# Splitting a mixer's narrow products by output rows over the two halves of TensorE's columns

## The chip, the cores and the metric

The kernel runs on one core of one Trainium2 chip. The metric is the time of one launch in microseconds (us), as the median of several runs. A profiled execution also gives a trace: one record for every instruction on TensorE (PE for products, PEld for the loads of its stationary operand), VectorE (DVE), ScalarE (ACT), GpSimd (POOL) and SyncE (SP).

## The reference

Two blocks of two layers each work on 256 tokens of width 1024 in fp32. The first block (dilated and differential attention, then windowed attention) is not touched by the change. Each layer of the second block mixes four branches and then runs a gated feed-forward net:

```python
for layer in range(DEPTH):                       # DEPTH = 2
    h = rms_norm_2(x, norm1_g[layer])
    y_sb = stick_breaking_attention(...)         # 4 heads of 64
    y_rwkv, v_first = rwkv7_time_mix(...)        # causal, 4 heads of 64
    y_moba = moba_attention(...)
    y_hgrn = hgrn2_mixer(...)                    # causal, 4 heads of 64
    for n, y_n in enumerate((y_sb, y_rwkv, y_moba, y_hgrn)):
        merged += sigmoid(h @ w_gate[n]) * (y_n @ w_branch[layer, n])
    x = x + merged @ w_out[layer]
    h2 = rms_norm_2(x, norm2_g[layer])
    x = x + (silu(h2 @ w_ffn_gate) * (h2 @ w_ffn_up)) @ w_ffn_down
```

The two causal mixers, rwkv7 and hgrn2, are linear recurrences that are computed chunk by chunk. In rwkv7 a chunk of 128 tokens needs the inverse of a unit triangular 128x128 matrix for each head.

## The kernel before

Weights come from HBM in units of 128x1024 fp32 (`unit`, L210): SP issues the load, ACT rounds the unit to `wh` (L220), and DVE forms the rest `wl` (L221). A projection is then three TensorE products for each pair of tiles (`mm3`, L236 to L240), with a moving operand of 512 or 256 columns in the rounded type. These are the L238, L239 and L240 of the profile, and they are most of the work.

The mixers run between the projections of a layer. `mixer_layer` (L1525) weaves two generators: `Rwkv.run` on one side, and on the other the attention branches, hgrn (L1102) and their projections. A scheduler orders each engine's instructions by priority before the launch, so TensorE's order is fixed, and mixer products stand in it between groups of projection products that don't depend on them.

All mixer products are in full fp32; each such product is two records on PE and two on PEld in the trace. The ones that matter here have a stationary operand of 128x128 and a moving operand of only 64 columns (or 2):

- `Rwkv.run` inverts the triangular matrices by doubling, six levels for 2 chunks and 4 heads. One level is: `p1` (L1409, 8 products), copied by ACT to `t1` (L1410); `p3` (L1415, 8 products), merged by DVE into `Y` (L1416); then transposes of `Y` into `px` (L1422), copied by ACT to `X`.
- After it, for each chunk: `pr` (L1433), copied to `R`; `pu` (L1444), copied to `R`; `pst` (L1451, L1452) for the state, in the first chunk only; and `py` (L1463, L1465). Earlier, `pn` (L1284) and `pb` (L1315) sum over heads with 2 columns.
- hgrn builds its scores over seven levels. `hs` (L1138) is the product of a level, DVE merges it (L1140) and updates `hq` (L1148) and `key` (L1149), which the next level's `hs` reads. At the end `ho` (L1166 to L1168) applies the scores to the values, 12 products of 64 columns.

Two places of the kernel already write to one half of the output partitions at a time, with a stationary operand of 128x64: `pst`, and the value products `pv` of the attentions (L373, L987, L989). `HALF` is the pair of slices 0:64 and 64:128. Scores (L364) use 64 rows of the contraction instead.

Of the kernel before, what the change touches and what calls it, by code (L numbers as in the profile page):

```python
# [95 lines left out]
HALF = (slice(0, 64), slice(64, 128))  # L96
# [3 lines left out]
class Net:  # L100
# [50 lines left out]
    def mm(self, name="mm"):  # L151
        t = self.p_mm.tile([128, 512], F32, name=name, tag="mm")
        return t
# [195 lines left out]
    def norm_rows(self, t, g, out, done=None):  # L349

        r = self.norm_stat(t, out)
        for j in range(2):
            s = slice(j * 512, j * 512 + 512)
            self.nc.vector.scalar_tensor_tensor(out[:, s], self.x[:, t, s], r, g[:, s], op0=OP.mult, op1=OP.mult)
            if done:
                done(j, s)


    def products(self, of):

# [599 lines left out]
def zsel(ap, b, z):  # L960

    return ap.rearrange("p (n z b) -> p n z b", z=2, b=b)[:, :, z, :]
# [139 lines left out]
def hgrn(n, l, q, f, key, it, sg, yT, c0):  # L1102


    nc = n.nc
    mm = nc.tensor.matmul
    lb, om = n.lb[:, l * 2:l * 2 + 2], n.omlb[:, l * 2:l * 2 + 2]
    nom = n.nomlb[:, l * 2:l * 2 + 2]
    heads = (slice(0, 64), slice(64, 128))
    for p in range(2):  # L1110
        nc.vector.tensor_scalar(key[:, p, :], f[:, p, :], nom[:, p:p + 1], om[:, p:p + 1], op0=OP.mult, op1=OP.add)
        nc.vector.tensor_scalar(f[:, p, :], f[:, p, :], om[:, p:p + 1], lb[:, p:p + 1], op0=OP.mult, op1=OP.add)
    fl = lambda t: t.rearrange("p a b -> p (a b)")
    kf, ff = fl(key), fl(f)

    sc = n.big("scb")
    yield
    for t in range(2):
        ps = n.mx("hs")
        s = slice(t * 128, t * 128 + 128)  # L1120
        for p in range(2):
            mm(ps[:, p * 256:p * 256 + 256].rearrange("p (a b) -> p a b", a=2), lhsT=key[:, p, s], rhs=q[:, p, :, s],
               start=True, stop=True)
        nc.vector.tensor_tensor(v4(sc[:, t * 512:t * 512 + 512]), v4(ps), bc(n.ident.unsqueeze(1), [128, 4, 128]),
                                op=OP.mult)
    for par, r in enumerate(heads):
        nc.vector.tensor_mul(q[r, :, par, :], q[r, :, par, :], f[r, :, :])
    yield
    tot, b = ff, 1
    for lv in range(7):  # L1130

        ps = n.mx("hs")
        for t in range(2):
            s = slice(t * 128, t * 128 + 128)
            for p in range(2):
                o = ps[:, t * 256 + p * 128:t * 256 + p * 128 + 128]
                qz = q[:, p, :, s].rearrange("p a (n z b) -> p a n z b", z=2, b=b)[:, :, :, 1, :]
                mm(o.rearrange("p (a n b) -> p a n b", a=2, b=b), lhsT=key[:, p, s], rhs=qz, start=True, stop=True)  # L1138
        m = bc(zsel(n.msk[:, lv, :], b, 1).unsqueeze(1), [128, 8, 64 // b, b])
        nc.vector.copy_predicated(sc.rearrange("p (g n z b) -> p g n z b", g=8, z=2, b=b)[:, :, :, 1, :], m,  # L1140
                                  ps.rearrange("p (g n b) -> p g n b", g=8, b=b))
        nb = 512 // (2 * b)
        kv = kf.rearrange("p (n z c) -> p n z c", z=2, c=b)
        tv = tot.rearrange("p (n z) -> p n z", z=2)
        for par, r in enumerate(heads):
            qv = q[r, :, par, :].rearrange("p g (n z c) -> p g n z c", z=2, c=b)[:, :, :, 1, :]
            tp = tv[r, :, 0:1].rearrange("p (g n) z -> p g n z", g=2)
            nc.vector.tensor_tensor(qv, qv, bc(tp, [64, 2, nb // 2, b]), op=OP.mult)  # L1148
        nc.vector.tensor_tensor(kv[:, :, 0, :], kv[:, :, 0, :], bc(tv[:, :, 1:2], [128, nb, b]), op=OP.mult)  # L1149
        nt = n.s2("tot", tag="tot")[:, :nb]  # L1150
        nc.vector.tensor_tensor(nt, tv[:, :, 0], tv[:, :, 1], op=OP.mult)
        tot, b = nt, 2 * b
        yield
    scx = n.s2("scx", tag="tm")
    ps = n.mx("hs")
    for p in range(2):
        mm(ps[:, p * 256:p * 256 + 256].rearrange("p (a b) -> p a b", a=2), lhsT=key[:, p, 0:128],
           rhs=q[:, p, :, 128:256], start=True, stop=True)
    nc.scalar.copy(scx, ps)
    yield  # L1160
    po = n.mx("ho")
    for h in range(4):
        o0, o1 = po[:, h * 64:h * 64 + 64], po[:, 256 + h * 64:256 + h * 64 + 64]
        c = slice(h * 64, h * 64 + 64)
        hs = slice(h * 128, h * 128 + 128)
        mm(o0, lhsT=sc[:, hs], rhs=it[:, 0, c], start=True, stop=True)  # L1166
        mm(o1, lhsT=scx[:, hs], rhs=it[:, 0, c], start=True, stop=False)
        mm(o1, lhsT=sc[:, 512 + h * 128:640 + h * 128], rhs=it[:, 1, c], start=False, stop=True)  # L1168
    o = n.s2("ho", tag="tm")
    nc.scalar.copy(o, po)  # L1170
    sq = n.s2("hsq", tag="tm")
    nc.scalar.activation(sq, po, AF.Square)
    yield
    ss = n.col(8, "ss")
    nc.vector.tensor_reduce(ss, sq.rearrange("p (a b) -> p a b", a=8), axis=AX.X, op=OP.add)
    r = n.rstd(ss, 64, 1e-6, 8)
    ov = o.rearrange("p (a b) -> p a b", a=8)
    nc.vector.tensor_tensor(ov, ov, bc(r.unsqueeze(2), [128, 8, 64]), op=OP.mult)
    nc.vector.tensor_mul(o, o, sg)
    with n.lazily(LATE):  # L1180
        for t in range(2):
            n.to_T(o[:, t * 256:t * 256 + 256], t, yT, c0, 2)
    yield


class Rwkv:
# [25 lines left out]
    def run(self, yT, c0):  # L1212
        n, nc, l = self.n, self.n.nc, self.l
        mm = nc.tensor.matmul
        col = lambda name, p: n.ccol(name, l * 2 + p, 1)
        r, k, v, wag = (self.x[i] for i in range(4))
# [7 lines left out]
        for p in range(2):  # L1224
            s = slice(p * 256, p * 256 + 256)
            c = slice(p * 128, p * 128 + 128)
# [9 lines left out]
        for t in range(2):  # L1236
            mm(pg[:, t * 256:t * 256 + 256], lhsT=lw[:, 1, t * 128:t * 128 + 128], rhs=self.wa[:, 256:512],
               start=True, stop=True)
# [6 lines left out]
        else:  # L1245
# [11 lines left out]
            for p in range(2):  # L1257
                s = slice(p * 256, p * 256 + 256)
                mm(pvm[:, s], lhsT=v12[0:32, 64 + p * 128:64 + p * 128 + 128], rhs=vl[0:32, 0:256],
                   start=True, stop=True)  # L1260
# [7 lines left out]
        for t in range(2):  # L1268
            for p in range(2):
                o = t * 256 + p * 128  # L1270
                nc.tensor.transpose(pvt[:, o:o + 128], v[:, p, t * 128:t * 128 + 128], n.ident)
        vt = n.s2("vt", tag="rl")
# [6 lines left out]
        sq = n.s2("kksq", tag="rt")  # L1279
        nc.scalar.activation(sq, flat(kk), AF.Square)  # L1280
        pn = n.mx("pn")
        for t in range(2):
            for p in range(2):
                mm(pn[:, t * 4 + p * 2:t * 4 + p * 2 + 2], lhsT=sq[:, p * 256 + t * 128:p * 256 + t * 128 + 128],  # L1284
                   rhs=n.cst[:, C_HALVES:C_HALVES + 128:64], start=True, stop=True)
        yield
        rn = n.col(8, "rn")
# [24 lines left out]
        pb = n.mx("pb")  # L1312
        for t in range(2):
            for p in range(2):
                mm(pb[:, t * 4 + p * 2:t * 4 + p * 2 + 2], lhsT=bn[:, p, t * 128:t * 128 + 128],  # L1315
                   rhs=n.cst[:, C_HALVES:C_HALVES + 128:64], start=True, stop=True)
        bon = n.col(8, "bon")
        nc.vector.tensor_copy(bon, pb[:, 0:8])
# [82 lines left out]
        for lv in range(1, 7):  # L1401

            z = 1 << lv
            half = lambda t, h: t[:, h * 64:h * 64 + 64].rearrange("p (n b) -> p n b", b=z)
            p1 = {}
            for c in range(2):
                p1[c] = n.mx("p1")
                for h in range(4):
                    mm(half(p1[c], h), lhsT=aT(c, h), rhs=zsel(X[c][:, hd(h)], z, 0), start=True, stop=True)  # L1409
                nc.scalar.copy(zsel4(t1[c], z, 0), run4(p1[c][:, 0:256], z))  # L1410
            yield
            for c in range(2):
                p3 = n.mx("p3")
                for h in range(4):
                    mm(half(p3, h), lhsT=t1[c][:, hd(h)], rhs=zsel(Y[c][:, hd(h)], z, 1), start=True, stop=True)  # L1415
                nc.vector.copy_predicated(zsel4(Y[c], z, 1), mask4(n, lv, z, 1), run4(p3[:, 0:256], z))  # L1416
            yield
            if lv < 6:
                for c in range(2):
                    px = n.mx("px")  # L1420
                    for h in range(4):
                        nc.tensor.transpose(px[:, hd(h)], Y[c][:, hd(h)], n.ident)  # L1422
                    nc.scalar.copy(X[c], px)
                yield
# [4 lines left out]
        for c in range(2):  # L1429

            pr_ = n.mx("pr")
            for h in range(4):
                mm(pr_[:, h * 64:h * 64 + 64], lhsT=aTk(c, h), rhs=vt[:, c * 256 + h * 64:c * 256 + h * 64 + 64],  # L1433
                   start=(h == 0), stop=(h == 3 and c == 0), skip_group_check=True)
            if c:
                for p in range(2):
                    mm(pr_[:, p * 128:p * 128 + 128], lhsT=ar[c][:, p * 256:p * 256 + 128],
# [3 lines left out]
            nc.scalar.copy(R[:, 0:256], pr_[:, 0:256])  # L1441
            pu = n.mx("pu")
            for h in range(4):
                mm(pu[:, h * 64:h * 64 + 64], lhsT=Y[c][:, hd(h)], rhs=R[:, h * 64:h * 64 + 64], start=True, stop=True)  # L1444
            nc.scalar.copy(R[:, 256:512], pu[:, 0:256])
            if c == 0:
                pst = n.mx("pst")
# [12 lines left out]
            py = n.mx("py")  # L1460
            for h in range(4):
                o = py[:, h * 64:h * 64 + 64]
                mm(o, lhsT=bT(c, h), rhs=R[:, 256 + h * 64:320 + h * 64], start=(h == 0), stop=False,  # L1463
                   skip_group_check=True)
                mm(o, lhsT=bTk(c, h), rhs=vt[:, c * 256 + h * 64:c * 256 + h * 64 + 64], start=False,  # L1465
                   stop=(h == 3 and c == 0), skip_group_check=True)
            if c:
                for p in range(2):
                    mm(py[:, p * 128:p * 128 + 128], lhsT=ar[c][:, p * 256 + 128:p * 256 + 256],
# [257 lines left out]
```

## Time and profile before

| | |
|---|---|
| median of 3 runs | 1330.22 us (1329.13 to 1332.9) |
| the profiled execution, own time | 1330.19 us |
| its span, first to last instruction | 1328.4 us |
| PE busy | 1270.1 us, 96% |
| PEld busy | 1082.6 us, 81% |
| DVE, ACT, POOL busy | 850.6 (64%), 645.3 (49%), 67.9 us (5%) |
| mean granted TensorE clock | 0.984 |

A record on PE lasts longer than it keeps the engine from the next one, because products are pipelined; what a product costs is read from the distance between starts. Times in a timeline are in us from the span's start, and a row may merge several records of one line, with their count behind the x.

### The profile page before, as it was taken

Reading aid. Unit: us, or ns where it says so; the run is one execution under the profiler, and the core shown is the slowest. Engines: PE = TensorE matmul, PEld = TensorE weight load, DVE = VectorE, ACT = ScalarE, POOL = GpSimd, SP = SyncE. Lnnn points to the kernel's source line nnn. Section 1 sums busy time; section 2 is a strip of 40 time slices with the busy share of each in tenths; the row PEclk is TensorE's granted clock in tenths of the full one; section 3 lists DMA queues with packets and bytes.
Section 4 is the critical chain, followed back from the end, with each engine's and each line's share of the span. In section 5 each row is a group of like instructions: output and inputs, shape, how many; then the busy total and the mean of one; then the engine's idle time right before and its main releaser. Section 6 shows DMA issues by size and latency. Waiting matters only on the chain.

```text
span 1328.4 us, 20159 instructions
## 1 busy us (share of the span) xinstructions
PE 1270.1 (96%) x7760; PEld 1082.6 (81%) x7760; DVE 850.6 (64%) x1456; ACT 645.3 (49%) x1083; POOL 67.9 (5%) x82
## 2 busy tenths in 40 slices
PE   6988889999899999999999999999999999999997
PEld 4857667977797888888899987987888887999986
DVE  6876897676758765666655544658754756655543
ACT  3353545675665335445544443555345544644432
POOL 0011110000001000000000000001000000000000
PEclk8989999999999999999999999999999999999999
DMA  8977755654563314365566654653232564666652
GB/s 318 328 249 263 244 178 184 209 156 128 150 191 96 98 59 133 115 203 180 177 191 185 186 183 155 211 163 95 80 109 67 169 199 156 206 185 181 190 185 86
DMA packets 104957, 227.19 MB, mean 171 GB/s; under 512 B 8207, under 2 KB 8351, under 8 KB 104861
## 3 DMA queue, kind: packets, MB, share of 16 engines
q1 hardware_dynamic: 102560, 219.18, 52.9%
q0 software_dynamic: 1984, 6.60, 1.8%
q8 instruction: 61, 1.00, 0.3%
q14 instruction: 36, 0.29, 0.1%
q10 hardware_dynamic: 316, 0.12, 0.0%
HBM read 224.82 MB, written 1.05 MB: 170 GB/s over the span
## 4 chain that ended last, share of the span: by engine, by line
PE 75%; DVE 5%; issue 5%; DMA 2%; ACT 2%; POOL 1%; DVEq 0%; POOLq 0%; ACTq 0%
PE mm L240 20%; PE mm L238 20%; PE mm L239 20%; DMA aw<-in_ada_w_dram 2%; PE p L1409 2%; PE p L1415 2%; PE hs L1138 1%; PE sc L364 1%; DVE wl L221 1%; PE pv L373 1%; DVE macc L447 1%; ACT wh L220 1%; PE pt L393 1%; PE px L1422 1%; PE cm L364 1%
## 5 line engine op out<-in xcount | busy, mean ns | idle before, releaser
L221 DVE TENSOR_TENSOR wl<-wr,wh 128x1024 fp32r<-128x1024 f32 (+1 forms) x372 | 430.9, 1165 | 266.0 <-ACT wh L220 262.6
L220 ACT CAST wh<-wr 128x1024 fp32r<-128x1024 f32 (+1 forms) x372 | 369.9, 1003 | 400.1 <-PE mm L240 164.2
L238 PE MATMUL mm<-hh,wh 128*128 128x256 f32 x1168 | 333.7, 287 | 0.9 <-ACT hh L321 0.9
L239 PE MATMUL mm<-hl,wh 128*128 128x256 f32 x1168 | 333.9, 286 | 0.0
L240 PE MATMUL mm<-hh,wl 128*128 128x256 f32 x1168 | 332.7, 285 | 0.0
L238 PEld LDWEIGHTS mm<-hh,wh 128*128 128x128 f32 x1168 | 225.4, 194 | 4.5 <-issue 2.4
L239 PEld LDWEIGHTS mm<-hl,wh 128*128 128x128 f32 x1168 | 225.4, 193 | 2.4 <-issue 2.2
L240 PEld LDWEIGHTS mm<-hh,wl 128*128 128x128 f32 x1168 | 225.3, 193 | 2.4 <-issue 2.3
L240 PE MATMUL mm<-wh,hl 128*128 128x512 f32 (+1 forms) x448 | 177.4, 396 | 0.3 <-DVE hl L322 0.3
L238 PE MATMUL mm<-wh,hh 128*128 128x512 f32 (+1 forms) x448 | 177.1, 396 | 0.6 <-ACT hh L321 0.4
L239 PE MATMUL mm<-wl,hh 128*128 128x512 f32 (+1 forms) x448 | 176.2, 393 | 0.4 <-DVE wl L221 0.4
L238 PEld LDWEIGHTS mm<-wh,hh 128*128 128x128 f32 x448 | 85.0, 190 | 18.0 <-ACT hh L321 1.3
L239 PEld LDWEIGHTS mm<-wl,hh 128*128 128x128 f32 x448 | 85.1, 190 | 17.6 <-DVE wl L221 0.8
L240 PEld LDWEIGHTS mm<-wh,hl 128*128 128x128 f32 x448 | 85.0, 190 | 17.0 <-DVE hl L322 1.2
L239 PE MATMUL mm<-wl,ff 128*128 128x512 f32 x176 | 69.5, 395 | 0.0
L238 PE MATMUL mm<-wh,ff 128*128 128x512 f32 x176 | 69.5, 395 | 0.0
L240 PE MATMUL mm<-wh,ff 128*128 128x512 f32 x176 | 69.4, 395 | 0.0
L447 DVE SCALAR_TENSOR_TENSOR macc<-aw,cs,macc 128x512 f32<-128x512 f32 x78 | 57.3, 745 | 13.7 <-DMA aw<-in_ada_w_dram 13.1
L239 PE MATMUL mm<-wl,yTh 128*128 128x512 f32 x128 | 50.9, 399 | 2.0 <-DVE wl L221 2.0
L240 PE MATMUL mm<-wh,yTl 128*128 128x512 f32 x128 | 50.5, 396 | 0.0
L238 PE MATMUL mm<-wh,yTh 128*128 128x512 f32 x128 | 50.0, 394 | 0.0
L384 ACT ACTIVATE p<-p,nm 128x256 f32<-128x256 f32 (+1 forms) x80 | 39.6, 496 | 18.7 <-DVE nm L381 18.1
(392 smaller groups left out, 1617.3 us busy)
## 6 DMA issues: line engine op xcount, KB each, us to landing
wr<-in_w_in_dram SPq DMA_DIRECT2D x120, 512.0 KB, 3.8
wr<-in_gu_dram SPq DMA_DIRECT2D x88, 512.0 KB, 3.8
wr<-in_w_ffn_down_dram SPq DMA_DIRECT2D x44, 512.0 KB, 3.7
aw<-in_ada_w_dram SPq DMA_DIRECT2D x80, 256.0 KB, 4.5
wr<-in_ab_w_in_dram SPq DMA_DIRECT2D x32, 512.0 KB, 5.3
wr<-in_c_w_in_dram SPq DMA_DIRECT2D x20, 512.0 KB, 4.1
wr<-in_w_branch_dram SPq DMA_DIRECT2D x16, 512.0 KB, 3.8
wr<-in_w_out_dram SPq DMA_DIRECT2D x16, 512.0 KB, 3.9
```

The costliest lines, as they stand in the source:

```text
L220: nc.scalar.copy(hi[:, i:i + m], raw[:, i:i + m])
L221: nc.vector.tensor_sub(lo[:, i:i + m], raw[:, i:i + m], hi[:, i:i + m].bitcast(F32))
L238: mm(out, lhsT=ah, rhs=bh, start=start, stop=False, **kw)
L239: mm(out, lhsT=ah, rhs=bl, start=False, stop=False, **kw)
L240: mm(out, lhsT=al, rhs=bh, start=False, stop=stop, **kw)
L364: self.nc.tensor.matmul(out, lhsT=lhsT, rhs=rhs, start=True, stop=True)
L373: self.nc.tensor.matmul(ps[HALF[hh], :], lhsT=vs(hh, kc), rhs=pTs[hh][:, kc * 256:kc * 256 + 256], start=(kc == 0), stop=(kc == 1))
L384: nc.scalar.activation(p, p, AF.Exp, bias=nm, scale=-1.0, accum_out=l)
L393: nc.tensor.transpose(ps[:, kc * 256 + t * 128:kc * 256 + t * 128 + 128], p[:, t, kc * 128:kc * 128 + 128], self.ident)
L447: nc.vector.scalar_tensor_tensor(acc, w, n.cs[:, k:k + 1], acc, op0=OP.mult, op1=OP.add)
L1409: mm(half(p1[c], h), lhsT=aT(c, h), rhs=zsel(X[c][:, hd(h)], z, 0), start=True, stop=True)
L1415: mm(half(p3, h), lhsT=t1[c][:, hd(h)], rhs=zsel(Y[c][:, hd(h)], z, 1), start=True, stop=True)
```

## The change

A new helper, `halves`, issues a product as two: one for output rows 0 to 63 and one for rows 64 to 127. Both read the same moving operand; each loads 64 columns of the stationary operand. The products of `ho`, `pn`, `pb`, `p1`, `p3`, `pr` (without its two products with the state), `pu` and `py` (likewise) go through it, 296 in both layers.

```diff
+    def halves(self, out, lhsT, rhs, **kw):
+        for r in HALF:
+            self.nc.tensor.matmul(out[r], lhsT=lhsT[:, r], rhs=rhs, **kw)
...
-        mm(o0, lhsT=sc[:, hs], rhs=it[:, 0, c], start=True, stop=True)
-        mm(o1, lhsT=scx[:, hs], rhs=it[:, 0, c], start=True, stop=False)
-        mm(o1, lhsT=sc[:, 512 + h * 128:640 + h * 128], rhs=it[:, 1, c], start=False, stop=True)
+        n.halves(o0, sc[:, hs], it[:, 0, c], start=True, stop=True)
+        n.halves(o1, scx[:, hs], it[:, 0, c], start=True, stop=False)
+        n.halves(o1, sc[:, 512 + h * 128:640 + h * 128], it[:, 1, c], start=False, stop=True)
...
-                mm(pn[:, t * 4 + p * 2:t * 4 + p * 2 + 2], lhsT=sq[:, p * 256 + t * 128:p * 256 + t * 128 + 128],
+                n.halves(pn[:, t * 4 + p * 2:t * 4 + p * 2 + 2], lhsT=sq[:, p * 256 + t * 128:p * 256 + t * 128 + 128],
...
-                    mm(half(p1[c], h), lhsT=aT(c, h), rhs=zsel(X[c][:, hd(h)], z, 0), start=True, stop=True)
+                    n.halves(half(p1[c], h), lhsT=aT(c, h), rhs=zsel(X[c][:, hd(h)], z, 0), start=True, stop=True)
...
-                    mm(half(p3, h), lhsT=t1[c][:, hd(h)], rhs=zsel(Y[c][:, hd(h)], z, 1), start=True, stop=True)
+                    n.halves(half(p3, h), lhsT=t1[c][:, hd(h)], rhs=zsel(Y[c][:, hd(h)], z, 1), start=True, stop=True)
...
-                mm(pr_[:, h * 64:h * 64 + 64], lhsT=aTk(c, h), rhs=vt[:, c * 256 + h * 64:c * 256 + h * 64 + 64],
-                   start=(h == 0), stop=(h == 3 and c == 0), skip_group_check=True)
+                n.halves(pr_[:, h * 64:h * 64 + 64], aTk(c, h), vt[:, c * 256 + h * 64:c * 256 + h * 64 + 64],
+                         start=(h == 0), stop=(h == 3 and c == 0), skip_group_check=True)
...
-                mm(pu[:, h * 64:h * 64 + 64], lhsT=Y[c][:, hd(h)], rhs=R[:, h * 64:h * 64 + 64], start=True, stop=True)
+                n.halves(pu[:, h * 64:h * 64 + 64], lhsT=Y[c][:, hd(h)], rhs=R[:, h * 64:h * 64 + 64], start=True, stop=True)
...
-                mm(o, lhsT=bT(c, h), rhs=R[:, 256 + h * 64:320 + h * 64], start=(h == 0), stop=False,
-                   skip_group_check=True)
+                n.halves(o, bT(c, h), R[:, 256 + h * 64:320 + h * 64], start=(h == 0), stop=False,
+                         skip_group_check=True)
```

`pb` changes as `pn` does, and the second product of `py` as the first. In the changed file every line behind the helper stands 5 lines lower, and split products all have the helper's line, L362.

The order on TensorE shows where the split products stand. First, one doubling level of the first mixer layer before, `p1` of both chunks between two groups of `hs` (p_4800 and p_4806 are the two PSUM tiles named p1):

```order
L1138 MATMUL hs<-hq,key 128x128
L1409 MATMUL p_4800<-X,ab 128x64 x4
L1409 MATMUL p_4806<-X,ab 128x64 x4
L1138 MATMUL hs<-hq,key 128x128 x3
L240 MATMUL mm<-wh,hl 128x512
```

The same place after the change:

```order
L1143 MATMUL hs<-hq,key 128x128
L362 MATMUL p_4856<-X,ab 64x64 x8
L362 MATMUL p_4866<-X,ab 64x64 x8
L1143 MATMUL hs<-hq,key 128x128 x3
L239 MATMUL mm<-wl,hh 128x512
```

The 8 products became 16 halves that follow each other without anything between, the two halves of a product side by side; before and behind them stand full-width products, as before.

Second, the end of hgrn in the same layer before (`ho` begins at L1166):

```order
L239 MATMUL mm<-wl,hh 128x512
L1157 MATMUL hs<-hq,key 128x256
L1415 MATMUL p_4817<-Y,t_4596 128x64 x4
L1415 MATMUL p_4823<-Y,t_4597 128x64 x4
L1157 MATMUL hs<-hq,key 128x256
L1166 MATMUL ho<-hi,scb 128x64
L1422 MATMUL px<-cst,Y 128x128 x8
L1167 MATMUL ho<-hi,scx 128x64
```

And after:

```order
L238 MATMUL mm<-wh,hh 128x512
L1162 MATMUL hs<-hq,key 128x256
L362 MATMUL p_4881<-Y,t_4604 64x64 x8
L362 MATMUL p_4891<-Y,t_4605 64x64 x8
L1162 MATMUL hs<-hq,key 128x256
L362 MATMUL ho<-hi,scb 64x64
L1427 MATMUL px<-cst,Y 128x128 x8
L362 MATMUL ho<-hi,scb 64x64
L362 MATMUL ho<-hi,scx 64x64 x2
```

`p3` is again one run of 16. The first product of `ho` has been parted: one half stands ahead of the eight transposes into `px` and the other behind them.

Third, the last level before, where `pt` are transposes of another branch:

```order
L1409 MATMUL p_5073<-X,ab 128x64 x4
L1409 MATMUL p_5079<-X,ab 128x64 x4
L240 MATMUL mm<-wh,hl 128x512
L1094 MATMUL pt<-cst,p 128x128
L1415 MATMUL p_5093<-Y,t_4596 128x64 x4
L1415 MATMUL p_5099<-Y,t_4597 128x64 x4
L1094 MATMUL pt<-cst,p 128x128 x5
```

And after:

```order
L362 MATMUL p_5173<-X,ab 64x64 x8
L362 MATMUL p_5183<-X,ab 64x64 x8
L1099 MATMUL pt<-cst,p 128x128 x2
L362 MATMUL p_5201<-Y,t_4604 64x64 x8
L1099 MATMUL pt<-cst,p 128x128
L362 MATMUL p_5211<-Y,t_4605 64x64 x8
L1099 MATMUL pt<-cst,p 128x128 x2
L992 MATMUL pv<-pT,vs 64x256
L362 MATMUL pr<-vt,ak 64x64 x8
```

Here the two chunks' `p3` now have a transpose between them, and the transposes of `pt` have moved ahead of and between them; `pr` follows a `pv` product, which also writes half of the output partitions. On SP the order is the same in both; on DVE, ACT and POOL some instructions of the mixers stand a few places earlier or later, and none is added or removed.

## Rows read from the trace of the kernel before

**Rows 1.** The page: the span and its first section, PE.

```profile
span 1328.4 us, 20159 instructions
...
PE 1270.1 (96%) x7760; PEld 1082.6 (81%) x7760; DVE 850.6 (64%) x1456; ACT 645.3 (49%) x1083; POOL 67.9 (5%) x82
```

**Rows 2.** Stretches of the first mixer layer and behind: busy time of each engine, TensorE's clock.

```profile
core 0: us, PE busy (x) PEld busy (x) DVE busy (x) ACT busy (x) POOL busy (x), PEclk, DMA share, GB/s
...
400.00:440.00 40.00, 37.47 (x242) 29.22 (x241) 32.32 (x64) 21.07 (x38) 5.20 (x5) 1.00 0.33 97
440.00:540.00 100.00, 99.39 (x638) 83.68 (x637) 59.41 (x132) 43.11 (x85) 4.25 (x6) 1.00 0.29 86
540.00:860.00 320.00, 317.73 (x1925) 282.73 (x1924) 188.08 (x213) 150.19 (x191) 6.40 (x8) 1.00 0.60 183
```

**Rows 3.** Groups by shape on PE: busy us, mean ns of one, idle before.

```profile
L1409 PE MATMUL p<-X,ab 128*128 128x64 f32 x192 | 23.7, 271 | 0.0
L1415 PE MATMUL p<-Y,t 128*128 128x64 f32 x192 | 23.4, 271 | 0.0
...
L1465 PE MATMUL py<-vt,ak 128*128 128x64 f32 x32 | 6.2, 275 | 0.0
...
L1168 PE MATMUL ho<-hi,scb 128*128 128x64 f32 x16 | 3.1, 275 | 0.0
...
L1315 PE MATMUL pb<-cst,bn 128*128 128x2 f32 x16 | 2.2, 240 | 1.5 <-DVE bn L1310 0.7 <-ACT beta L1009 0.7
```

**Rows 4.** Timeline of PE in py: start, length, line, records.

```profile
529.92 0.39 PE L1463 MATMUL py<-R,ab 128*128 128x64 f32 x2
...
530.82 0.39 PE L1463 MATMUL py<-R,ab 128*128 128x64 f32 x2
```

**Rows 5.** Timeline of PE in the second layer's pst.

```profile
1018.26 0.34 PE L1451 MATMUL pst<-R,bk 128*64 128x64 f32 x4
...
1018.66 0.33 PE L1452 MATMUL pst<-vt,bk 128*64 128x64 f32 x4
1018.92 0.33 PE L1094 MATMUL pt<-cst,p 128*128 128x128 f32 x1
```

**Rows 6.** Timeline of PE around single pv halves, first and second layer.

```profile
531.26 0.61 PE L1433 MATMUL pr<-vt,ak 128*128 128x64 f32 x4
531.80 0.65 PE L987 MATMUL pv<-pT,vs 128*64 128x256 f32 x2
532.38 0.66 PE L1433 MATMUL pr<-vt,ak 128*128 128x64 f32 x4
532.88 0.66 PE L1437 MATMUL pr<-st,ar 128*128 128x128 f32 x4
...
908.24 0.39 PE L240 MATMUL mm<-wh,hl 128*128 128x512 f32 x1
908.56 0.65 PE L987 MATMUL pv<-pT,vs 128*64 128x256 f32 x2
...
909.47 0.39 PE L239 MATMUL mm<-wl,hh 128*128 128x512 f32 x1
909.70 0.39 PE L240 MATMUL mm<-wh,hl 128*128 128x512 f32 x1
```

**Rows 7.** Timeline of PE, the last three of four pv products in a row.

```profile
314.81 0.82 PE L373 MATMUL pv<-pT,v 128*64 128x256 f32 x6
```

**Rows 8.** Timeline of one level: hs, p1, hs, DVE's chain, the next hs.

```profile
463.04 0.46 PE L1138 MATMUL hs<-hq,key 128*128 128x128 f32 x2
463.33 1.90 PE L1409 MATMUL p<-X,ab 128*128 128x64 f32 x16
...
465.07 0.89 PE L1138 MATMUL hs<-hq,key 128*128 128x128 f32 x6
...
465.99 0.71 DVE L1140 COPY_PREDICATED scb<-msk,hs 128x512 f32<-128x512 uint8 x1 [2.87 <-PE hs L1138]
...
467.45 0.42 DVE L1149 TENSOR_TENSOR key<-key,tot 128x256 f32<-128x256 f32 x1
...
468.02 0.46 PE L1138 MATMUL hs<-hq,key 128*128 128x128 f32 x2
```

More of the change, by code (lines that the diff above doesn't have):

```diff
@@ L1314, in run @@
             for p in range(2):
-                mm(pb[:, t * 4 + p * 2:t * 4 + p * 2 + 2], lhsT=bn[:, p, t * 128:t * 128 + 128],
+                n.halves(pb[:, t * 4 + p * 2:t * 4 + p * 2 + 2], lhsT=bn[:, p, t * 128:t * 128 + 128],
                    rhs=n.cst[:, C_HALVES:C_HALVES + 128:64], start=True, stop=True)
@@ L1462, in run @@
                 o = py[:, h * 64:h * 64 + 64]
-                mm(o, lhsT=bT(c, h), rhs=R[:, 256 + h * 64:320 + h * 64], start=(h == 0), stop=False,
-                   skip_group_check=True)
-                mm(o, lhsT=bTk(c, h), rhs=vt[:, c * 256 + h * 64:c * 256 + h * 64 + 64], start=False,
-                   stop=(h == 3 and c == 0), skip_group_check=True)
+                n.halves(o, bT(c, h), R[:, 256 + h * 64:320 + h * 64], start=(h == 0), stop=False,
+                         skip_group_check=True)
+                n.halves(o, bTk(c, h), vt[:, c * 256 + h * 64:c * 256 + h * 64 + 64], start=False,
+                         stop=(h == 3 and c == 0), skip_group_check=True)
             if c:
```

## The prediction

> **What bounds the kernel now.** I read the page first: PE is busy for 96% of the span [rows 1]. A busy share of PE says little alone, since its records overlap, so I went on to the stretches. The split products stand in the two mixer stages, in the first layer in 400 to 540 us, and with the same lines again in the second. [...]
>
> Next, the groups by shape: the products in question have a stationary operand of 128x128 and 64 moving columns, with no idle time before them (0.0 for L1409, L1415, L1465 and L1168); pb, with 2 columns, has 1.5 us [rows 3]. Counting all lines (two records a product): p1 and p3 96 products each, py 32, ho 24, pr and pu 16 each, pn and pb 8 each, together 296.
>
> **What such a product costs.** In py, eight records start from 529.92 up to 530.82, which begins the ninth: 0.90/8 = 0.112 us a record, 0.224 a product [rows 4]. It is the same in p1: 16 records last 1.90, less one record's 0.27, over 15 starts: 0.109 [rows 8]. 296 products are 66.3 us.
>
> **What the halves cost.** Before has two places that use half of the output rows. In pst, 16 records with 64 stationary and 64 moving columns take 0.66 us up to the next line's start [rows 5]. That is the work of four full products, which would take 0.90. Leaving this mode costs about 0.14 (below), so the 16 themselves take 0.52: 0.033 a record, 0.13 for what was one product. In pv, six records of 256 columns, alternating between the two halves as the change's do, last 0.82; less one record's 0.38 (its length in [rows 6], 0.65 for two that start 0.27 apart), that is 0.44 for the two steps between three pairs, so 0.22 a pair [rows 7]. If the halves ran one after the other, six such records would last 5 x 0.22 + 0.38 = 1.48. So two halves do run side by side, loads included.
>
> By these rows a split product costs between 0.112 (half of 0.224, pairs without a gap) and 0.13 (pst). I take 0.12, nearer to pairs, since pst carries the start of a run in its 16 records and most runs here have 32: saved are 296 x (0.224 - 0.12) = **30.8 us**.
>
> [...]
>
> **What the mode costs.** A pv product amid full-width ones shows it. From 531.26 to 532.88 stand 8 records of pr (8 x 0.112 = 0.90) and 2 of pv on one half (2 x 0.22); 1.62 - 0.90 - 0.44 = 0.28 is left for going in and out. Between projection products, 908.24 to 909.47 is 1.23, less 2 x 0.22 and two products of 0.23 (909.47 to 909.70): 0.33 [rows 6]. Without a change of form the next load lies under the running product; here it doesn't. In TensorE's order before, 40 stretches write half of the output rows; after, 83 do. Of the 43 more, 27 are followed by fp32 products or transposes and 16 by projection products: 27 x 0.28 + 16 x 0.33 = **12.9 us** lost. Some are pure loss: the single half of ho ahead of the px transposes, and p3 parted by a transpose in the last level, both shown in the order. Bounds: 0.25 and 0.35 for each, 10.8 to 15.1.
>
> **What is late next.** In a level, p1 stands between the first hs and the other three, and the next level's hs waits for DVE: hs from 465.07, L1140 at 465.99, L1149 from 467.45 to 467.87, hs at 468.02 [rows 8]. This chain (2.95 us) comes behind p1 in series, and the projection products that cover it stay behind hs in the order. A shorter p1 or p3 thus moves the whole chain forward; it uncovers nothing in it. The same holds for ACT's copy of p1, which has hs and nine projection products ahead of p3. Where p1 and p3 nearly touch (the last level, and pr to pu over the copy R) a few tenths can come out. pn and pb lie where PE waits anyway [rows 2, 3]: their 16 x 0.104 = 1.7 us may not arrive. I take **2 us** for all of this; bounds 0 and 4.8 (half of the second rival). Weights: SP's order is unchanged and no transfer is added, and DVE at 59% and ACT at 43% have room to round them for a stage that is 8 us shorter in 100.
>
> **Sum.** 30.8 - 12.9 - 2 = 15.9 saved. The profiled execution took 1330.19 (span 1328.4 and 1.8 around it), which is the median, 1330.22, too. So 1330.2 - 15.9 = **1314 us**. With 0.112, 10.8 and 0: 33.2 - 10.8 = 22.4, 1308. With 0.13, 14.2 (all at 0.33) and 4.8: 27.8 - 19.0 = 8.8, 1321.
>
> **Rivals.**
> Slower: halves in long runs don't overlap, because TensorE is fed no faster than a half each 0.056. The evidence for pairs is short: 16 records in pst, 6 and 8 in pv, and before them PE stood on a wait or on long products, so that instructions could gather; runs of 32 records are new. For it: nothing in this trace shows more than 16 records at 0.033. Against it: each run has projection products ahead of it too, at 0.23 us a product, time to gather in. Then a product costs 0.224 as before, and the 12.9 is lost: 1343. The change loses once a product costs over 0.224 - 12.9/296 = 0.180, 0.045 a half record.
> [...]
>
> Waits: the levels are held by DVE and ACT. For it: hs follows L1149's end by 0.15 us, so there is no slack [rows 8]; if DVE's weight rounding comes between, p1's gain is waited away. Against it: DVE has 41% free. The 8 runs of p1 and p3 among hs in each layer would lose 8 x 0.104 - 0.28 = 0.55 each, 8.8 in all: 1323.
>
> No change: pairs overlap only in part, at about 0.17 to 0.19 a product: 1327 to 1333. That the change isn't made as written is excluded by the order: halves of a product stand next to each other.
>
> **Chances.** 1314 as forecast (1308 to 1321) 0.62; waits (to 1326) 0.16; slower 0.12; no change 0.07; still better, if pairs are exact and runs also meet, 0.03. The range 1305 to 1326 holds the first two and part of the last, 0.80. A measurement of this kernel tells a change of about 0.3%, 4 us. Faster 0.79, same 0.09, slower 0.12.
>
> **What the profile would show.** L362 with 1184 records (296 x 4) in place of 592; a run of 32 p1 records from its first start to the next hs in 0.9 to 1.2 us, where 1.74 stood; 0.27 to 0.35 more than the bare work for each run's way in and out; from one level's hs to the next some 0.5 us less than the 4.98 from 463.04 to 468.02; stretches 440 to 540 shorter by 7 to 8, all else equal. I am wrong if starts within a run come at 0.05 us or more a record, or if PE's idle time ahead of hs, p3 or pu grows by more than 5 us in both layers.

## The result

The changed kernel takes **1311.2 us** (median of 4 runs, 1308.83 to 1314.01), the kernel before 1330.83 beside it (1329.13 to 1332.9): a ratio of 0.9853, 95% interval 0.9828 to 0.9877. Timed once more beside the last experiment, it took 1313.93 against 1331.44, ratio 0.9865 [0.984, 0.9889]. The profiled execution took 1311.63, with a span of 1309.9. The forecast was 1314, range 1305 to 1326. One execution of a kernel below (everything else) took 2442.69 us, nearly twice as long as its others, and is left out.

The page of the changed kernel, its span and the line of PE, against [rows 1]:

```profile
span 1309.9 us, 21345 instructions
...
PE 1250.9 (95%) x8352; PEld 1055.4 (81%) x8352; DVE 851.1 (65%) x1456; ACT 644.3 (49%) x1083; POOL 67.2 (5%) x82
```

PE has 592 records more (two for each of 296 products) and 19.2 us less busy time; the other engines do what they did. The groups by shape, against [rows 3]; the columns are busy us, mean ns of one, idle before:

```profile
L362 PE MATMUL p<-X,ab 128*64 128x64 f32 x384 | 15.2, 226 | 0.0
L362 PE MATMUL p<-Y,t 128*64 128x64 f32 x384 | 15.0, 226 | 0.0
...
L362 PE MATMUL py<-vt,ak 128*64 128x64 f32 x64 | 3.9, 222 | 0.0
...
L362 PE MATMUL pb<-cst,bn 128*64 128x2 f32 x32 | 1.6, 201 | 1.5 <-DVE bn L1315 0.8 <-ACT beta L1014 0.7
```

Twice the records, and yet less busy time: 15.2 for 23.7 in p1. A record is hardly shorter (226 ns for 271), so the time can only be saved by records that lie beside each other. The idle time of 1.5 before pb is what it was.

The timeline of a doubling level of the first layer, against [rows 8], PE and DVE (start, length, line, records; PEld and projection products left out):

```profile
456.85 0.46 PE L1143 MATMUL hs<-hq,key 128*128 128x128 f32 x2
...
457.24 1.15 PE L362 MATMUL p<-X,ab 128*64 128x64 f32 x32
...
458.32 0.94 PE L1143 MATMUL hs<-hq,key 128*128 128x128 f32 x6
...
459.29 0.71 DVE L1145 COPY_PREDICATED scb<-msk,hs 128x512 f32<-128x512 uint8 x1 [2.37 <-PE hs L1143]
...
460.75 0.43 DVE L1154 TENSOR_TENSOR key<-key,tot 128x256 f32<-128x256 f32 x1
...
461.33 0.46 PE L1143 MATMUL hs<-hq,key 128*128 128x128 f32 x2
```

The run of p1 lasts 458.32 - 457.24 = 1.08 up to the next hs, where 1.74 stood. 32 records are (1.15 - 0.22)/31 = 0.030 apart, 0.12 a product. The way in shows ahead of it: 0.39 from hs to p1, where 0.29 stood. From hs to hs the level takes 4.48 us for 4.98. DVE's chain has moved forward as a whole: hs follows the end of L1154 (460.75 + 0.43) by 0.15, as before.

The timeline of py, against [rows 4], each row four records or one product:

```profile
517.89 0.29 PE L362 MATMUL py<-vt,ak 128*64 128x64 f32 x4
518.01 0.29 PE L362 MATMUL py<-R,ab 128*64 128x64 f32 x4
...
518.59 0.29 PE L362 MATMUL py<-vt,ak 128*64 128x64 f32 x4
518.71 0.28 PE L362 MATMUL pr<-vt,ak 128*64 128x64 f32 x2
```

Seven products in 518.71 - 517.89 = 0.82: 0.117 each, for 0.224 before. What PE waited for in the first layer's mixers, first in the trace of before (440 to 540), then in that of the changed kernel (440 to 530); the columns are us in total, times, longest:

```profile
engine line waited for: us in total, times, longest us
PE hs L1138 <- DVE key L1149: 0.6, 1, 0.6
```

```profile
engine line waited for: us in total, times, longest us
PE hs L1143 <- DVE key L1154: 0.6, 1, 0.6
```

One wait of 0.6 us in each, for the same update of `key`. No wait has taken the place of what was saved.

**A measure for the mixers.** The whole program varies by several us from run to run, most of it ahead of the mixers (the first pn starts between 393.0 and 399.8 us in these kernels' profiles). So I read a stretch that repeats: from the first product cm, which comes behind pn and pb, to the last record of py, in both layers. Its ends in the first layer of the changed kernel:

```profile
413.71 0.48 PE L369 MATMUL cm<-ar,kk 64*128 64x256 f32 x1
```

```profile
524.53 0.71 PE L1474 MATMUL py<-st,ar 128*128 128x128 f32 x4
525.00 0.48 PE L239 MATMUL mm<-wl,hh 128*128 128x512 f32 x1
```

What must be put right is work that crosses the marks: the scheduler places a few more or fewer projection products between the same two marks. The changed kernel has 438 of 512 columns there and the kernel before 443, so 5 x 0.229 us have only moved behind the mixers. The same is done for the few transposes pt that cross a mark, at 0.11. One run of six pv records crosses too. In the second layer of the kernel before it stands behind products of cm, inside the stretch:

```profile
915.42 0.43 PE L987 MATMUL pv<-pT,vs 128*64 128x256 f32 x1
915.42 0.43 PE L989 MATMUL pv<-pT,vs 128*64 128x128 f32 x2
915.68 0.38 PE L987 MATMUL pv<-pT,vs 128*64 128x256 f32 x1
915.90 0.38 PE L989 MATMUL pv<-pT,vs 128*64 128x128 f32 x2
916.21 0.50 PE L240 MATMUL mm<-wh,hl 128*128 128x512 f32 x1
```

It takes 916.21 - 915.42 = 0.79 up to the next product, of which some 0.7 are its own by the prices on record (0.22 for the pair of 256 columns, half of that for each of two pairs of 128, 0.28 for its way in and out). In the changed kernel it has joined another run of pv ahead of the first cm, so that 0.7 leave the stretch without being saved; the same holds for all kernels below but p1 and p3 alone and the two with pn and pb whole.

For the changed kernel: 235.7 us before, 218.6 after, 17.1 less, of which 0.9 (1.14 of products out, 0.22 of transposes in) and the 0.7 of pv have moved: **15.5 us saved**; in its second profile 15.6. Counted from the first pn, pt and pv lie inside with either kernel and only eight projection products leave: 277.16 - 259.33 - 8 x 0.229 = 16.0, with pn and pb in it. The expectations below count from the first pn (277.2 before, 259.3 after), without any correction, since I found both flaws only later; the second one, the clock ahead of cm, is shown at the last experiments.

### The profile page after: what moved, and what is told of

Same layout as the page of the kernel before. It is cut to its first block, busy times and chain, and to the rows that moved or that the text cites. A ratio compares the mean times of both kernels' runs of the same rounds, so it can differ in the third digit from the quotient of the medians.

```text
span 1309.9 us, 21345 instructions
## 1 busy us (share of the span) xinstructions
PE 1250.9 (95%) x8352; PEld 1055.4 (81%) x8352; DVE 851.1 (65%) x1456; ACT 644.3 (49%) x1083; POOL 67.2 (5%) x82
## 4 chain that ended last, share of the span: by engine, by line
PE 71%; DVE 6%; issue 5%; DMA 2%; ACT 2%; POOL 1%; DVEq 0%; POOLq 0%; ACTq 0%
PE mm L240 20%; PE mm L239 20%; PE mm L238 20%; PE p L362 2%; PE hs L1143 1%; DVE wl L221 1%; PE sc L369 1%; PE pv L378 1%; ACT wh L220 1%; DMA wr<-in_gu_dram 1%; DMA wr<-in_w_in_dram 1%; PE px L1427 1%; DMA aw<-in_ada_w_dram 1%; PE pt L398 1%; DVE macc L452 1%
## 5 line engine op out<-in xcount | busy, mean ns | idle before, releaser
L238 PE MATMUL mm<-hh,wh 128*128 128x256 f32 x1168 | 333.9, 288 | 0.9 <-ACT hh L321 0.9
L240 PE MATMUL mm<-hh,wl 128*128 128x256 f32 x1168 | 332.9, 286 | 0.0
L238 PEld LDWEIGHTS mm<-hh,wh 128*128 128x128 f32 x1168 | 225.5, 194 | 4.5 <-issue 2.4
L240 PEld LDWEIGHTS mm<-hh,wl 128*128 128x128 f32 x1168 | 225.5, 193 | 2.7 <-issue 2.6
L240 PE MATMUL mm<-wh,hl 128*128 128x512 f32 (+1 forms) x448 | 176.2, 394 | 0.9 <-DVE hl L322 0.9
L238 PE MATMUL mm<-wh,hh 128*128 128x512 f32 (+1 forms) x448 | 175.4, 392 | 0.6 <-ACT hh L321 0.4
L240 PEld LDWEIGHTS mm<-wh,hl 128*128 128x128 f32 x448 | 84.5, 189 | 18.9 <-DVE hl L322 2.3
L238 PEld LDWEIGHTS mm<-wh,hh 128*128 128x128 f32 x448 | 84.6, 189 | 17.5 <-ACT hh L321 1.7
L238 PE MATMUL mm<-wh,ff 128*128 128x512 f32 x176 | 69.5, 395 | 0.0
L240 PE MATMUL mm<-wh,ff 128*128 128x512 f32 x176 | 69.4, 395 | 0.0
L240 PE MATMUL mm<-wh,yTl 128*128 128x512 f32 x128 | 50.5, 396 | 0.0
L238 PE MATMUL mm<-wh,yTh 128*128 128x512 f32 x128 | 50.0, 395 | 0.1
L389 ACT ACTIVATE p<-p,nm 128x256 f32<-128x256 f32 (+1 forms) x80 | 39.6, 496 | 17.5 <-DVE nm L386 16.7
```

Source lines behind the costliest of these rows:

```text
L238: mm(out, lhsT=ah, rhs=bh, start=start, stop=False, **kw)
L240: mm(out, lhsT=al, rhs=bh, start=False, stop=stop, **kw)
L389: nc.scalar.activation(p, p, AF.Exp, bias=nm, scale=-1.0, accum_out=l)
```

## The experiments

Only the changed lines are shown; `n.full` issues a product whole, as before. The stretches and what they come to stand in one table behind the experiments.

**p1 and p3 alone.** Split are only the 192 products of p1 and p3.

```diff
-        n.halves(o0, sc[:, hs], it[:, 0, c], start=True, stop=True)
+        n.full(o0, sc[:, hs], it[:, 0, c], start=True, stop=True)
...
-                n.halves(pn[:, t * 4 + p * 2:t * 4 + p * 2 + 2], lhsT=sq[:, p * 256 + t * 128:p * 256 + t * 128 + 128],
+                n.full(pn[:, t * 4 + p * 2:t * 4 + p * 2 + 2], lhsT=sq[:, p * 256 + t * 128:p * 256 + t * 128 + 128],
```

(likewise for the other products of ho, for pb, pr, pu and py.)

> Only p1 and p3 (192 of 296 products) are split. Theory 'pairs' (two halves side by side, 0.12 us a product instead of 0.224, and 0.28 us, or 0.33 beside projection products, for each way in and out of writing half the rows): 192 x 0.104 = 20.0 saved, 24 more ways before fp32 work and 8 before projection products cost 9.4, so 10.6 us less than before: about 1320. Rival 'order' (the gain comes from the new order of work on TensorE, not from the halves' price): p1 and p3 runs keep 0.22 a product in the trace, and the time is anywhere, likeliest the 1311 of the change. In the trace a run of 32 p1 records should again take about 1.08 us to the next hs.

Measured: 1319.76 us (1317.52 to 1320.21), ratio 0.9917 [0.9895, 0.994]; from pn to py 267.0. A run of 32 p1 records takes 1.08 us to the next hs again (460.21 to 461.29). The 104 other products carry part of the gain, so the order alone, which hardly differs from the change's, is not what brings it.

**Everything else.** The opposite: p1 and p3 whole, the other 104 split.

> p1 and p3 whole again, the other 104 products split. If the terms add up product by product and way by way: 104 x 0.104 = 10.8 saved, less 1 way at 0.28 and 10 at 0.33 = 3.6, so 7.2 against before and some 1323 us; the mixer stages, from the first pn to the last py, 277.2 - 7.2 = 270. Together with the run that splits p1 and p3 alone it should give the change's own gain, 10.2 + 7.2 = 17.4 against 17.9 in the stages. Rival: the short runs (8 records of pr, 4 of pn, single halves of ho) don't pay for their way in and out, and the stages are within 2 us of before, some 1330 us.

Measured: median 1324.96 of nine executions (1320.25 to 1330.42), ratio 0.9965 [0.9944, 0.9986]; from pn to py 271.1, 6.1 less than before, with four projection products more in it, so 7.0 for the same work, near the 7.2 expected; by the measure above 6.5. Short runs pay too. The two parts make 8.6 + 6.5 = 15.1 of the change's 15.5.

**Heads by turns.** In p1 and p3 heads 0 and 2 are split and heads 1 and 3 are whole, so each product has a way in and out of its own.

```diff
-                    n.halves(half(p1[c], h), lhsT=aT(c, h), rhs=zsel(X[c][:, hd(h)], z, 0), start=True, stop=True)
+                    (n.full if h % 2 else n.halves)(half(p1[c], h), lhsT=aT(c, h), rhs=zsel(X[c][:, hd(h)], z, 0), start=True, stop=True)
```

(and the same in p3.)

> As the change, but in p1 and p3 heads 1 and 3 stay whole, so that split and whole products alternate. Theory 'pairs' with a price of about 0.3 us on each way in and out: 200 products split save 20.8, 108 more ways cost 98 x 0.28 + 10 x 0.33 = 30.7, so about 10 us slower than before: 1340. Rival 'covered' (going in and out is hidden under running products and the 0.28 read from single pv products was something else): half of p1's and p3's saving goes, 1311 + 10 = 1321.

Measured: 1344.97 us (1342.99 to 1347.17), ratio 1.011 [1.0081, 1.0139], slower than before the change. The timeline of this kernel in a p3 of the first layer, PE only:

```profile
457.77 0.34 PE L362 MATMUL p<-Y,t 128*64 128x64 f32 x4
458.04 0.43 PE L366 MATMUL p<-Y,t 128*128 128x64 f32 x2
458.40 0.34 PE L362 MATMUL p<-Y,t 128*64 128x64 f32 x4
458.67 0.43 PE L366 MATMUL p<-Y,t 128*128 128x64 f32 x2
...
460.20 0.90 PE L1147 MATMUL hs<-hq,key 128*128 128x128 f32 x6
```

One split and one whole product take 458.40 - 457.77 = 0.63. Bare, by py's 0.117 and by the 0.109 a record of a whole one [rows 8], they would take 0.117 + 0.218; 0.295 is left for one way in and out. It shows in both steps: 0.36 behind the whole product, 0.27 behind the split one.

**Upper halves first.** In p1 and p3 the upper halves of all four heads stand ahead of their lower halves: the same records, but neighbours write the same half.

```diff
-                for h in range(4):
-                    n.halves(half(p1[c], h), lhsT=aT(c, h), rhs=zsel(X[c][:, hd(h)], z, 0), start=True, stop=True)
+                for r in HALF:
+                    for h in range(4):
+                        mm(half(p1[c], h)[r], lhsT=aT(c, h)[:, r], rhs=zsel(X[c][:, hd(h)], z, 0), start=True, stop=True)
```

(and the same in p3.)

> As the change, but in p1 and p3 the four heads' upper halves stand ahead of the four lower halves, so that 8 records of one half stand ahead of the first of the other. Theory 'pairs, looking ahead' (TensorE takes a product of the free half from at least 8 records further on, as it took one from 4 further on in pst): as the change, 1311, within 4. Rival 'neighbours' (only halves next to each other run side by side): p1 and p3 fall back to 0.224 a product and keep their ways in and out, 192 x 0.104 = 20 lost: 1331.

Measured: 1324.36 us (1320.94 to 1326.55), ratio 0.9956 [0.9942, 0.9971], between the two. A p1 of the first layer, PE only:

```profile
461.60 0.46 PE L1143 MATMUL hs<-hq,key 128*128 128x128 f32 x2
461.99 1.54 PE L1415 MATMUL p<-X,ab 128*64 128x64 f32 x32
463.46 0.94 PE L1143 MATMUL hs<-hq,key 128*128 128x128 f32 x6
```

The run takes 1.47 us: 1.08 with the halves side by side, 1.74 for whole products. The single records say why. I read the first eight as those of one half: from the second on, each starts 0.058 us after the one before it. But at the fifth of them a record starts only 6 ns after another (462.267 and 462.273), and from there two rows of starts, each 0.058 apart, run beside each other for a few records (462.380 and 462.384, 462.438 and 462.442). The second row would be the other half's: its first record, the ninth in program order, starts while three of the first eight still wait. So the halves overlap here too, but only over the last three records of a group. The trace names no half in a record, so this rests on the pattern of starts and on one sign more: the record that updates p1's semaphore for the first chunk, in the changed kernel the sixteenth and last of that chunk's, is the nineteenth to start here.

**Quarters.** p1 and p3 in four products of 32 output rows.

```diff
+    def quarters(self, out, lhsT, rhs, **kw):
+        for q in range(4):
+            r = slice(q * 32, q * 32 + 32)
+            self.nc.tensor.matmul(out[r], lhsT=lhsT[:, r], rhs=rhs, **kw)
...
-                    n.halves(half(p1[c], h), lhsT=aT(c, h), rhs=zsel(X[c][:, hd(h)], z, 0), start=True, stop=True)
+                    n.quarters(half(p1[c], h), lhsT=aT(c, h), rhs=zsel(X[c][:, hd(h)], z, 0), start=True, stop=True)
```

> As the change, but p1 and p3 are split into four products of 32 output rows. If a half record's 0.056 is the time of streaming 64 columns twice over, four quarters side by side also take 0.056 each and a product 0.112 to 0.12: as the change, 1311, within 4. If instead TensorE is fed a record each 0.028 to 0.030 us, and the halves have just met that, eight records cost 0.23 to 0.24 a product, and the 192 products give back 192 x 0.115 = 22: 1333. If loads were what bounded a half, quarters would be faster than the change: 192 x 0.05 = 10, 1301.

Measured: 1314.47 us (1312.52 to 1319.62), ratio 0.9887 [0.9856, 0.9918]. A p1 of the first layer, PE only:

```profile
458.38 0.46 PE L1149 MATMUL hs<-hq,key 128*128 128x128 f32 x2
458.77 1.10 PE L368 MATMUL p<-X,ab 128*32 128x64 f32 x64
459.80 0.94 PE L1149 MATMUL hs<-hq,key 128*128 128x128 f32 x6
```

64 records in (1.10 - 0.22)/63 = 0.014 us each: twice as many as with halves, in the same time (a run of 1.03 for 1.08). So nothing that feeds TensorE binds a run of halves. Four quarters take 0.056, about what two halves do (0.117/2 in py), though each loads half as many columns of the stationary operand. What is left to bind, I take it, is the stream of the 64 moving columns; a fixed least time of some 0.056 for a record in its own output rows would give the same here, and no run with quarters and another number of columns tells the two apart.

By the measure above this kernel saves 15.2, no more than the change: PE's idle time in the stretches grew by 2.1 us, from 1.8 to 3.9. In its second layer the trace shows what PE waited for (903 to 1012 us):

```profile
PE hs L1149 <- DVE key L1160: 1.2, 2, 0.6
...
PE tr L1067 <- ACT t L1421: 0.4, 1, 0.4
```

The wait for `key` comes twice where it came once, and one for ACT's copy is new. That is the forecast's rival "waits", in a kernel whose runs are a little shorter or whose order differs a little; which of the two, I did not try.

**hs too.** The 56 products of hs with 128 moving columns are split as well.

```diff
-                mm(o.rearrange("p (a n b) -> p a n b", a=2, b=b), lhsT=key[:, p, s], rhs=qz, start=True, stop=True)
+                n.halves(o.rearrange("p (a n b) -> p a n b", a=2, b=b), lhsT=key[:, p, s], rhs=qz, start=True, stop=True)
```

> hs split as well, a stationary operand of 128x128 with 128 moving columns (256 in the last level). By the reading that the stream of a half's columns binds: 64 columns took 0.056 us, so 128 take 0.112, a pair of halves takes 0.112, a product 0.224 as it does whole, and nothing is saved; the ways change by 6 fewer ahead of fp32 products and 14 more ahead of projections, 14 x 0.33 - 6 x 0.28 = 2.9 lost: 1314 us, the stages 259.3 + 2.9 = 262.2. Rival: halving the output rows halves any product, because the load binds: the 56 products of hs save 0.11 each, 6.2, less 2.9: 1308 us, the stages 256.

Measured: 1314.5 us (1308.06 to 1317.4), ratio 0.9874 [0.9842, 0.9906]; from pn to py 260.6, between the two expectations and nearer to 262.2. An hs of three products, PE only:

```profile
455.76 0.96 PE L362 MATMUL hs<-hq,key 128*64 128x128 f32 x12
456.65 0.50 PE L240 MATMUL mm<-wh,hl 128*128 128x512 f32 x1
```

12 records are (0.96 - 0.28)/11 = 0.062 us apart (0.28 is one half record's length later in this trace): 0.25 a product, no less than a whole one, (0.89 - 0.28)/5 = 0.122 a record by the six of [rows 8]. So with 128 columns nothing is halved. By the measure above the kernel saves 14.2, 1.3 less than the change.

**A preference for order.** While the halves of a product are issued, the scheduler is given an urgency, which keeps a run together: no single half of ho ahead of the px transposes, no transpose inside the last p3. Three kernels: pn and pb whole without it, the same with it, and the change with it.

```diff
+        with self.lazily(-20000):
+            for r in HALF:
+                self.nc.tensor.matmul(out[r], lhsT=lhsT[:, r], rhs=rhs, **kw)
```

pn and pb whole, without it:

> pn and pb whole, all else as in the change. Split, their 16 products save 16 x 0.104 = 1.7 and cost 1 way ahead of fp32 products and 4 ahead of projections, 0.28 + 1.32 = 1.6: nothing to be seen, stages 259.2 to 259.4, some 1311 us. Rival: these products lie in PE's waits, so that splitting them brought nothing and the ways were hidden with them: the same time. If instead the ways are paid and the products' gain is not, the stages are 1.6 shorter, 257.7.

The same with it:

> pn and pb whole, and a preference in the scheduler that keeps the halves of a run together (no single half of ho ahead of the px transposes, no transpose inside the last p3): 57 ways ahead of fp32 products and 17 ahead of projections, against 58 and 25. By the price of a way: 280 x 0.104 = 29.1 less 26 x 0.28 + 8 x 0.33 = 9.9, so 19.2 saved in the stages against 17.9 with the change, 258.0 against 259.3, and some 1310 us, which the total alone can't tell from the change. Rival: the ways saved lay under waits, or the other order makes a mixer result late: the stages at 260 or more.

The change with it:

> The change as it is (pn and pb split too) with the scheduler's preference that keeps the halves of a run together: 61 ways ahead of fp32 products and 18 ahead of projections, against 58 and 25. By the price of a way 7 x 0.33 - 3 x 0.28 = 1.5 less than the change in the mixer stages: 257.8 against 259.3. If what splitting pn and pb brought (1.0 between the runs with and without it) and what the order brought (1.1) simply add up: 258.2. In the total some 1 us, less than its measurement tells. Rival: the two don't add up, because the ways saved lay beside waits: the stages at 259 or more.

Measured: 1314.48 (ratio 0.9882 [0.9856, 0.9907]), 1314.99 (0.9885 [0.9862, 0.9907]) and 1313.77 (0.9868 [0.9845, 0.9892]); from pn to py 260.2, 259.3 and 261.5. The first lies 0.8 above what was expected, the second between its theory and its rival, and the last where its rival has it. But the trace of the last shows another cause, ahead of cm. Stretches of it in the first layer; the number behind the five engines' busy times, PEclk, is TensorE's granted clock:

```profile
395.00:400.00 5.00, 3.16 (x28) 2.28 (x26) 3.44 (x12) 1.39 (x4) 2.32 (x2) 1.00 0.37 107
400.00:405.00 5.00, 4.53 (x32) 4.31 (x33) 4.37 (x15) 2.22 (x3) 0.05 (x1) 0.57 0.02 3
405.00:410.00 5.00, 5.00 (x34) 5.00 (x34) 5.00 (x13) 4.19 (x14) 0.00 (x0) 0.75 0.00 0
410.00:415.00 5.00, 5.00 (x39) 4.48 (x38) 5.00 (x10) 3.05 (x5) 3.15 (x2) 1.00 0.33 105
```

The granted clock was 0.57 from 400 to 405 us and 0.75 from 405 to 410. PE had been busy for 3.16 of the 5 us before. The changed kernel has 1.00 in that place, behind 5 us (393.35 to 398.35) with 3.45 busy. From the first pn to the first cm this kernel takes 23.6 us and the changed one 20.8. The first of the three has a clock of 0.68 in 885 to 890, between the second layer's pn and cm. So that stretch, in which PE waits for DVE and ACT, can differ by two us between profiles, and the measure begins at cm. From there on the order brought 16.0 against 16.0 with pn and pb whole, and 16.2 against 15.5 with them split, where the four ways saved had 1.3 by their price each time: about half of it at most.

What splitting pn brings is read in pn itself. Four products of the first layer, of the changed kernel and then of the kernel before:

```profile
392.95 0.63 PE L362 MATMUL pn<-cst,kksq 128*64 128x2 f32 x16
393.51 0.39 PE L239 MATMUL mm<-hl,wh 128*128 128x256 f32 x1
```

```profile
397.83 0.95 PE L1284 MATMUL pn<-cst,kksq 128*128 128x2 f32 x8
398.65 0.36 PE L239 MATMUL mm<-hl,wh 128*128 128x256 f32 x1
```

0.56 for 0.82, a gain of 0.26 with the way paid. Though only 2 columns are streamed, the halves are (0.63 - 0.20)/15 = 0.029 apart, 0.057 for two, nearly as with 64 columns (0.20 is a record's length in the groups above); and whole records with 2 columns are (0.95 - 0.24)/7 = 0.10 apart (0.24 by pb of [rows 3]), near the 0.109 of 64. So the stream does not bind here. What is left, I take it, is the load of the stationary operand: its records on PEld last 0.133 to 0.138 us in pn with 64 columns and 0.189 to 0.192 with 128. Over the way to the first cm in the first layer, both split take 20.8 and both whole 21.2, of which 0.23 is a projection product that moved: some 0.2 for pn and pb together.

**The change again.**

> The change itself once more, on the chip of the runs beside it, to see what its stages and its total repeat to. If the 4.8 us that the first profile of it gained ahead of the first pn belong to that execution and not to the change, the mixer stages are 259.3 again, within 0.3, the first pn comes between 395 and 400 us, and the median is some 1313 us, 17 to 18 under the kernel before. If they belong to the change, the first pn comes near 393 and the median is 1311.

Measured: 1313.93 us (1311.25 to 1316.17). The mixers repeat: 259.6 from pn to py, 218.4 from cm to py (218.6 the first time). The question ahead of them stays open: the first pn starts at 393.7, as early as in the first profile (393.0; 397.8 before), yet the median is that of the other case.

**All stretches together.** "Saved" is against the kernel before, from the first cm to the last py in both layers, with the moved projection products, transposes and pv taken out. "On record" is what the forecast's prices give for those stretches (0.104 a product, 0.28 and 0.33 a way); "read again" takes 0.101 a product (0.218 - 0.117) and 0.31 a way.

| kernel | cm to py, two layers | products of 512 columns in them | saved | on record | read again |
|---|---|---|---|---|---|
| before | 119.8 + 115.9 | 443 | | | |
| the change | 111.3 + 107.3 | 438 | 15.5 | 17.9 | 16.5 |
| the change again | 111.1 + 107.3 | 438 | 15.6 | 17.9 | 16.5 |
| p1 and p3 alone | 114.2 + 110.6 | 433 | 8.6 | 10.6 | 9.5 |
| everything else | 117.1 + 113.3 | 450 | 6.5 | 7.2 | 7.0 |
| heads by turns | 125.4 + 122.0 | 438 | -13.4 | -10.0 | -13.3 |
| hs too | 111.7 + 108.2 | 438 | 14.2 | 14.9 | 14.0 |
| pn, pb whole | 110.8 + 107.1 | 435 | 16.0 | 17.9 | 16.5 |
| the same, ordered | 110.7 + 107.2 | 435 | 16.0 | 19.2 | 17.7 |
| the change, ordered | 110.6 + 107.2 | 438 | 16.2 | 19.2 | 17.7 |
| upper halves first | 116.3 + 112.3 | 438 | 5.5 | | |
| quarters | 111.9 + 108.3 | 444 | 15.2 | | |

The prices that were read again explain seven rows within 1.0 us, and the two ordered kernels within 1.7; all but one of the nine save less than they say. None of the kernels beats the change by more than the measurement can tell.

## Why the prediction was right

**What set the pace: PE's stream.** Before, PE had a record in flight for 99.39 of the 100 us from 440 to 540, at a granted clock of 1.00, while DVE had 59.41 and ACT 43.11; in 400 to 440 it was 37.47 of 40 [rows 2]. In the changed kernel it is 89.23 of the 90 us from 440 to 530, at 1.00 again, with DVE at 57.95 and ACT at 41.26. So time taken from PE's stream came off the mixer stages: 15.5 by the measure above.

**What a product costs: right.** 0.12 was taken between bounds of 0.112 and 0.13; the trace has 0.117 (py) to 0.12 (p1, with the start of its run). The whole product was put a little high: 0.224, where runs of p1 give 0.109 a record, 0.218 [rows 8]. With 0.101 a product 29.9 are saved by 296, not 30.8.

**What the mode costs: right in kind, at least 0.4 us low.** 12.9 was 43 ways at 0.28 or 0.33; heads by turns show 0.295. At 0.101 a product the rows of the table with over thirty ways ask for 0.31 (heads by turns, hs too) to 0.36 (the ordered kernels); at 0.31 it is 13.3. With heads by turns the price is seen on both sides: two full-width records with the step into the next pair take 0.36, where they would take 0.218, and the pair's step out takes 0.27 for 0.117. The loads of the kernel before show the same around its single pv: L240's load starts at 908.02, 0.22 ahead of its product at 908.24, and the load of the L238 behind pv at 909.13, 0.01 ahead of its product at 909.14.

**What is late next: hardly anything, as argued, so the 2 us were not lost to waits.** The wait for `key` is 0.6 us in the first layer with either kernel, and PE's idle time in the stretches is 1.8 before and 2.3 or 2.1 in the change's two profiles. DVE's chain moved forward whole (0.15 from L1154 to hs both times), and the level became 0.50 shorter, as stated. Of pn and pb no more arrived than the 0.1 net of their prices promised, or a little: pn gains 0.26 for four products, both some 0.2 over the way to cm. (The bound of 4.8 for this term, called half of the second rival's 8.8, should have been 4.4; nothing hangs on it.)

**The sum.** 15.9 were forecast and 16.0 measured from the first pn on, but part by part 29.9 - 13.3 = 16.6, less some 0.4 of idle time, in place of 30.8 - 12.9 - 2. So the sum owes its closeness to three small errors that cancel. The medians fell by 19.6 and 17.5. The 1.5 to 3.6 beyond the mixers lie in stretches where the two kernels have the same work, but for the few products that moved; in the first profile the first pn alone came 4.9 earlier, in the second 4.1. The spans of the first two profiles differ by 18.5: 4.9 ahead of pn, 17.8 in the mixers, less 4.2 behind the two mixer stages, of which 1.8 are the projection products that moved there. Other kernels of these runs, with nearly the same work ahead of pn, have it anywhere from 394.6 to 399.8. Whether the change has a part in it is not settled.

**The rivals.** Slow feeding is refuted: 32 records come at 0.030 and 64 quarters at 0.014, where a half each 0.056 was feared. The point from which the change would lose, 0.180 a product with the mode's price lost, is far off; heads by turns show what losing looks like: 108 more ways than before for 200 split products, 1344.97 us. Waits beyond those of before came with quarters (2.1 us), and in tenths with hs split and with the ordered kernel whose pn and pb are whole. That pairs overlap only in part, at 0.17 to 0.19 a product, is refuted by the 0.117 of py.

## What to carry to other kernels

In this kernel an fp32 product with few moving columns costs the same with 2 as with 64 (0.10 and 0.109 a record), as if the load of its stationary operand bound it. Split by output rows into neighbours that write different rows, its records lie beside each other, and its price falls: 0.218 to 0.117 us at 64 columns, nothing at 128. Each way into half-width products and out again costs about 0.3 us (0.28 to 0.36 by the readings above), what three split products save: count the runs, not only the products, and keep the two halves next to each other, since with the upper halves of four heads first a run took 1.47 us in place of 1.08. Where a fixed order moves fillers across a mark, count the fillers before reading a stretch.

## What the hardware showed beside that

- Quarters start 0.014 us apart: four records of 32 rows take 0.056, two of 64 rows 0.117/2 in py.
- By the pattern of starts, a record for the other half overtakes up to three waiting ones (upper halves first, from 462.273 us on); the records of one half stand 0.057 to 0.058 apart, whether they stream 2 columns (pn) or 64.
- TensorE's clock was granted at 0.57 and 0.75 for ten us in one execution, behind a stretch in which PE was busy for 3.16 of 5 us, and at 1.00 in the same place of the first layer in the six profiles beside it whose clock was read there (before, the change twice, p1 and p3 alone, pn and pb whole without the order and with it), in the changed kernel behind 3.45 of 5.
